# Operand addresses of TensorE modulo 64 bytes in a one-core encoder trunk: one residue for all, low tiles moved

## The chip, the core and the metric

One core of a Trainium2 chip runs the whole program. The metric is the device time of one execution in microseconds (us), the median of the timed runs. For the kernel before that is 1330.88 us (three runs, 1330.51 to 1332.0). Five engines work in parallel, each with an instruction queue of its own: PE (TensorE, matmuls; its weight loads are listed apart as PEld), DVE (VectorE), ACT (ScalarE), POOL (GpSimd) and SP (which only issues DMAs here).

## What is computed

One layer of an encoder over 256 tokens of width 2048, in float32, cut here to its matmuls:

```python
h = rms_norm(x, g_norm)
proj = h @ w_in                                  # 2048 x 9216: u,v | q,k,v | two gates
y_a = gmlp_branch(uv, ln_g, ln_b, w_s, b_s)      # u * (W_s LN(v) + b), by 128-token chunks
y_b = neighbourhood_attn(q, k, v, rpb)           # 16 heads
merged = g_a * (y_a @ w_branch[:GM_WIDTH]) + g_b * (y_b @ w_branch[GM_WIDTH:])
x = x + merged @ w_out
up = conv3(rms_norm(x, g) @ w_up)                # 2048 x 11008, then a width-3 convolution over tokens
x = x + (silu(gate) * val) @ w_down              # 5504 x 2048
return rms_norm(x, norm_final)
```

## The kernel before

**Two parts for each operand.** Every big product is made from float32 operands split in two: a high part (rounded to the matmul's format, tiles `whi` and `half_hi` for weights, written by ACT at L245) and a low part, the rest (`wlo`, `half_lo`, written by DVE at L248). Three products are added in PSUM: high x high, high x low, low x high.

**Weights arrive in pieces.** All weight matrices lie in HBM in the order of use, cut into pieces of at most 512 KB. `load` sends one piece by one DMA from SP's queue into a free `wraw` tile (the first 16 pieces, which hold a part of x beside their weights, into `start` tiles). `prepare` splits pieces up to `AHEAD - 1` = 4 ahead of the one in use, each into a slot of two tiles, `whi` and `wlo`, of 128 partitions x 1024 elements. Slots 0 to 3 lie at the low end of SBUF; from the output projection on there are also slots 4 and 5 and the pair `half_hi`/`half_lo`, at the high end. A slot returns to the end of a list when its piece has been used. `begin(i)` loads, prepares, and then runs the tasks that were put down for piece i with `at(i, f)`; after it the matmuls of piece i follow. So the order of work on each engine is fixed by this loop.

**Kinds of groups.** In a matmul the moving operand is streamed (up to 512 columns) against a stationary operand of 128 x 128 that a LDWEIGHTS has loaded before.

- Weight-stationary groups (`ws_step`, `spread_products`): u, q/k and the up-projection. The weights are stationary, the activations `h` move. L349 multiplies a high weight tile with both parts of `h` (512 columns), L355 a low weight tile with the high part alone (256 columns). Even pieces run all highs first and then all lows, odd pieces lows first, so highs and lows come in runs of 16. There are 1760 of each; 1376 of each belong to the up-projection.
- Groups with moving weights (`three_products`, L364 to L366, 908 matmuls on each line, 512 columns): v, gates, branches, output projection, down-projection. Stationary are `h`, `y` (branch outputs), `m` (merged) or `a` and `s` (activations of the MLP).
- The first group (L381, L382, L384, 192 matmuls), v of the gMLP, whose pieces bring x.

**Down-projection.** Some pairs of its pieces are multiplied with seven products in place of eight; L301 to L304 build sums of weights, and `combine` (L460 to L463 and L958, DVE and ACT) adds the parts up afterwards, in three tasks that are put down for the three pieces after the pair. In the last group the last four pieces are multiplied output by output (`by_block`), so that each finished output can be normalised and stored while PE goes on.

**Start.** ACT's queue sends the x part of piece 0 and then the 8 KB of norm weights (`vec`, L548); SP sends the rest of piece 0 in two DMAs, and the next pieces. PE runs 14 transposes of the identity meanwhile (`WAKE`, L561).

**Addresses.** Where a tile starts in its partition, modulo 64 bytes (in the text: its residue), as the built program has it:

```
tile                                            before   after
whi, slots 0 to 3 (low end of SBUF)                  0      32
wlo, slots 0 to 3                                    0      32 (start of the tile)
h, a, s, m, wraw, start, ident (low end)             0      32
whi and wlo, slots 4 and 5 (high end)               32      32 (start of the tile)
half_hi, half_lo, y, x2 (high end)                  32      32
```

Before, all low-end tiles in this table stand at 256 modulo 512, all high-end ones at 480 modulo 512. Tiles are cut at multiples of 512 bytes for a matmul's operands.

Of the kernel before, what the change touches and what calls it, by code (L numbers as in the profile page):

```python
# [8 lines left out]
F32 = mybir.dt.float32  # L9
F32R = mybir.dt.float32r  # L10
# [5 lines left out]
T = 256  # L16
D = 2048
NT = T // 128
KD = D // 128
# [20 lines left out]
BLOCK = 1024  # L40
AHEAD = 5
RAW, UNITS, HALVES = 5, (4, 2), 1
WAKE = 14
EARLY = 4

FF_BLOCKS = ((0, 22), (22, 43))
FF_SEVEN = ((3, 5, 7), (2, 4, 6))
# [71 lines left out]
def weight_pieces():  # L119

    groups, order = weight_stream()
    out, count, at = [], {}, 0
    for key in order:
        _, w, pieces = groups[key]
        tiles, blocks = pieces[count.get(key, 0)]
        count[key] = count.get(key, 0) + 1
        cols = sum(n for _, n in blocks)
        out.append((key, w, tiles, blocks, at, cols))
        at += 128 * len(tiles) * cols
    return out, at  # L130
# [19 lines left out]
def trunk_kernel(ctx, tc, x, weights, vectors, ln_g, ln_b, w_s_turned, b_s, rpb, norm_final, out):  # L150
    nc = tc.nc
# [8 lines left out]
    def keep(name, side="left", bufs=1, space=None):  # L160
        p, st = pool(name, side, bufs, space)
        ctx.push(st)
        return p

    psum = keep("psum", space=PSUM)
    const = keep("const")
# [3 lines left out]
    ypool, y_st = pool("yT", "right")  # L170

    junk = tmp.tile([128, 512], F32, name="junk")

    banks = {n: None for n in range(8)}
    spare = list(range(8))

    def bank():
        n = spare.pop(0)
        banks[n] = psum.tile([128, 512], F32, name=f"bank{n}")
        return banks[n]  # L180
# [7 lines left out]
    pieces, _ = weight_pieces()  # L188
# [17 lines left out]
    def at(i, f):  # L206
        tasks.setdefault(i, []).append(f)
# [5 lines left out]
    def load():  # L213
        while n_loaded[0] < len(pieces):
            i = n_loaded[0]
            slots = start_free if i < KD else raw_free
            if not slots:
                return
            n_loaded[0] += 1
            for f in preload.pop(i, ()):  # L220
                f()
            _, _, tiles, _, off, cols = pieces[i]
            size = len(tiles) * cols
            slot = slots.pop(0)
            w = slot[0].tile([128, size if i < KD else BLOCK], F32, name=slot[1])
            for c0, c1 in ((T, 768), (0, T), (768, 1280)) if i == 0 else ((0, size),):
                queue = nc.scalar if (i, c0) == (0, 0) else nc.sync
                queue.dma_start(w[:, c0:c1], bass.AP(tensor=weights.tensor, offset=weights.offset + off + c0,
                                                       ap=[[size, 128], [1, c1 - c0]]))
            raw[i] = (w, slot)  # L230

    def raw_done(i):
        (start_free if i < KD else raw_free).append(raw.pop(i)[1])

    def unit(key):
        slot = unit_free.pop(0)
        h, l = (slot[0].tile([128, BLOCK], F32R, name=f"w{p}{slot[1]}") for p in ("hi", "lo"))
        units[key] = (h, l, slot)
        return h, l

    def unit_done(key):
        unit_free.append(units.pop(key)[2])

    def high(h, w):
        nc.scalar.activation(h, w, AF.Copy)  # L245

    def low(l, w, h):
        nc.vector.tensor_sub(l, w, h.bitcast(F32))  # L248

    def split_first(i):  # L250
        def go():
# [6 lines left out]
            else:  # L258
                nc.scalar.activation(dst[:, 0, :], x, AF.Copy, scale=g)
            nc.vector.scalar_tensor_tensor(dst[:, 1, :], x, g, dst[:, 0, :].bitcast(F32), op0=OP.mult,  # L260
                                           op1=OP.subtract)
            parts = ((0, 512), (512, 1024)) if i < EARLY else ((0, 1024),)
            for c0, c1 in parts:
# [5 lines left out]
    def split_piece(i):  # L269
        if i < KD:  # L270
            return split_first(i)

        def go():
            size = len(pieces[i][2]) * pieces[i][5]
            h, l = unit(i)
            w = raw[i][0]
            high(h[:, :size], w[:, :size])
            low(l[:, :size], w[:, :size], h[:, :size])
            raw_done(i)
        return go  # L280
# [38 lines left out]
    queue = []  # L319
# [104 lines left out]
    def wide_step(key, acts, sevens, rest, done, by_block=0):  # L424


        n0, size = starts[key], size_of[key]
        tiles = [pieces[n0 + n][2][0] for n in range(size)]
        firsts = [n for n in range(size) if n0 + n in seven]
        box, opened, left = {}, set(), {}  # L430
        OUT = {(0, 0): 2, (0, 1): 3, (1, 0): 4, (1, 1): 8}
        uses = []
        n = 0
        while n < size:
            if n in firsts:
                uses += [1, 2, 3, 5, 7, 6, 4]
                n += 2
            else:
                uses += list(OUT.values())
                n += 1  # L440
        for u in uses:
            left[u] = left.get(u, 0) + 1

        def p(u):
            if u not in box:
                box[u] = bank()
            return box[u]

        def product(u, x, w):
            start = u not in opened  # L450
            opened.add(u)
            left[u] -= 1
            three_products(p(u), x, w, start, left[u] == 0)

        def combine(i):

            nu, nv = (fx["p"].tile([128, 512], F32, name=f"comb{n}") for n in range(2))

            def one():
                nc.scalar.activation(nu, p(1), AF.Copy)  # L460
                rest(0, 0, nu, OP.add)
                nc.vector.tensor_sub(nu, nu, p(6))
                nc.vector.tensor_sub(nv, nu, p(7))  # L463
                free(p(1), p(6), p(7))

            def two():
                rest(0, 1, nu, OP.subtract)
                rest(0, 1, p(5), OP.add)
                rest(1, 0, nv, OP.add)

            def three():
                rest(1, 1, nv, OP.subtract)
                rest(1, 1, p(5), OP.add)
                free(p(5))

            for n, f in enumerate((one, two, three)):
                at(i + 1 + n, f)

        def step(i):
            n = i - n0  # L480
            c0, c1 = slice(0, 512), slice(512, 1024)
            if n in firsts:
                k = tiles[n]
                h, l, _ = halves[i]
                hb, lb, _ = units[i, "b"]
                product(1, acts(k, 0), (h, l))
                product(2, acts(k + 1, 0), (hb[:, c0], lb[:, c0]))
                product(3, sevens(k)[3], (hb[:, c1], lb[:, c1]))
                half_free.append(halves.pop(i)[2])
                unit_done((i, "b"))  # L490
            elif n - 1 in firsts:
                k = tiles[n - 1]
                ht, lt, _ = units[i - 1, "t"]
                hs, ls, _ = units[i - 1, "s"]
                S = sevens(k)
                product(5, S[0], (ht[:, c0], lt[:, c0]))
                product(7, S[2], (ht[:, c1], lt[:, c1]))
                unit_done((i - 1, "t"))
                product(6, S[1], (hs[:, c1], ls[:, c1]))
                product(4, acts(k + 1, 1), (hs[:, c0], ls[:, c0]))  # L500
                unit_done((i - 1, "s"))
                if n - 1 == firsts[-1]:
                    combine(i)
            elif n < size - by_block:
                h, l, _ = units[i]
                for (b, c), u in OUT.items():
                    cs = slice(c * 512, (c + 1) * 512)
                    product(u, acts(tiles[n], b), (h[:, cs], l[:, cs]))
                unit_done(i)
            elif n == size - 1:  # L510
                for b, c in ((0, 0), (1, 0), (0, 1), (1, 1)):
                    u = OUT[b, c]
                    for m in range(size - by_block, size):
                        h, l, _ = units[n0 + m]
                        cs = slice(c * 512, (c + 1) * 512)
                        product(u, acts(tiles[m], b), (h[:, cs], l[:, cs]))
                    done(p(u), b, c, i + 1)
                    free(p(u))
                for m in range(size - by_block, size):
                    unit_done(n0 + m)  # L520
            if n == size - 1 and not by_block:
                for (b, c), u in OUT.items():
                    done(p(u), b, c, i + 1)
                    free(p(u))
        return step
# [18 lines left out]
    vec = const.tile([128, 2 * KD + 8 * NF], F32)  # L544
    gmix, gffn = vec[:, :KD], vec[:, KD:2 * KD]
    ck = vec[:, 2 * KD:].rearrange("p (j f) -> p j f", j=4)
    load()
    nc.scalar.dma_start(gmix, vectors[:, :KD])  # L548

    one = const.tile([128, 1], F32)  # L550
    nc.vector.memset(one, 1.0)
# [10 lines left out]

    keep_awake(WAKE)
    free(wake)
# [588 lines left out]
    for n in range(len(FF_BLOCKS)):  # L1153
        for j in range(2):
            key = ("down", n, j)
# [110 lines left out]
    for i, piece in enumerate(pieces):  # L1266
        key = piece[0]
# [45 lines left out]
```

## Time and profile before

The profiled execution took 1331.57 us; its span, from the first to the last instruction, is 1329.1 us.

| engine | busy | instructions |
|---|---|---|
| PEld | 1116.5 us (84%) | 6778 |
| ACT | 728.8 us (55%) | 1072 |
| POOL | 100.3 us (8%) | 192 |

Weight DMAs on SP's queue move 252.33 MB and keep the 16 DMA engines 59.0% busy. "Busy" of PE is from the start of a matmul to its modelled end; matmuls overlap, so the pace of PE is read from the distance of two starts, not from the mean duration of one. A row of the timeline has the start in us from the span's start, the duration (of the merged instructions, if there are several, with their count behind x), engine, line, operation, output and inputs, and in brackets the idle time before it and what ended that. Buffer numbers are left out of its names.

### The profile page before, as it was taken

Reading aid. Unit: us, or ns where it says so; the run is one execution under the profiler, and the core shown is the slowest. Engines: PE = TensorE matmul, PEld = TensorE weight load, DVE = VectorE, ACT = ScalarE, POOL = GpSimd, SP = SyncE. Lnnn points to the kernel's source line nnn. Section 1 sums busy time; section 2 is a strip of 40 time slices with the busy share of each in tenths; the row PEclk is TensorE's granted clock in tenths of the full one; section 3 lists DMA queues with packets and bytes.
Section 4 is the critical chain, followed back from the end, with each engine's and each line's share of the span. In section 5 each row is a group of like instructions: output and inputs, shape, how many; then the busy total and the mean of one; then the engine's idle time right before and its main releaser. Section 6 shows DMA issues by size and latency. Waiting matters only on the chain.

```text
span 1329.1 us, 18475 instructions
## 1 busy us (share of the span) xinstructions
PE 1316.1 (99%) x6778; PEld 1116.5 (84%) x6778; DVE 945.4 (71%) x1362; ACT 728.8 (55%) x1072; POOL 100.3 (8%) x192
## 2 busy tenths in 40 slices
PE   9999999999999999999999999999999999999996
PEld 7888888888788888888888888888888888888885
DVE  5676667776564546565878777797858787869986
ACT  5855567576444444454655555554545555546553
POOL 0502065430000000000000000000000000000000
PEclk9999999999999999999999999999999999999999
DMA  8857676655556667665565656556656565546743
GB/s 327 321 177 208 195 218 191 203 151 190 180 182 189 190 189 255 204 189 187 171 203 174 200 179 199 180 175 220 207 190 190 191 187 194 183 135 222 249 147 127
DMA packets 73898, 261.40 MB, mean 197 GB/s; under 512 B 9552, under 2 KB 10832, under 8 KB 73296
## 3 DMA queue, kind: packets, MB, share of 16 engines
q1 hardware_dynamic: 69696, 252.33, 59.0%
q0 software_dynamic: 3680, 7.30, 2.0%
q8 instruction: 53, 0.87, 0.3%
q10 hardware_dynamic: 432, 0.60, 0.1%
q14 instruction: 37, 0.30, 0.1%
HBM read 256.00 MB, written 2.10 MB: 194 GB/s over the span
## 4 chain that ended last, share of the span: by engine, by line
PE 95%; DVE 3%; DMA 1%; ACT 1%; issue 0%; ACTq 0%; DVEq 0%
PE bank L349 30%; PE bank L355 16%; PE bank L364 14%; PE bank L366 14%; PE bank L365 14%; PE bank L381 1%; PE bank L382 1%; PE bank L384 1%; DVE wlo L248 1%; DMA wraw<-in_weights_dram 1%; PE bank L830 1%; ACT whi L245 0%; PE bank L882 0%; DMA vec<-in_vectors_dram 0%; PE bank L704 0%
## 5 line engine op out<-in xcount | busy, mean ns | idle before, releaser
L248 DVE TENSOR_TENSOR wlo<-wraw,whi 128x1024 fp32r<-128x1024 f32 (+1 forms) x466 | 561.2, 1217 | 231.1 <-ACT whi L245 223.5
L245 ACT ACTIVATE whi<-wraw 128x1024 fp32r<-128x1024 f32 (+1 forms) x466 | 481.1, 1046 | 285.2 <-PE bank L365 168.9
L349 PE MATMUL bank<-h,whi 128*128 128x512 f32 x1760 | 425.8, 392 | 0.0
L349 PEld LDWEIGHTS bank<-h,whi 128*128 128x128 f32 x1760 | 322.2, 188 | 64.1
L355 PEld LDWEIGHTS bank<-h,wlo 128*128 128x128 f32 x1760 | 225.3, 190 | 9.4
L355 PE MATMUL bank<-h,wlo 128*128 128x256 f32 x1760 | 229.5, 282 | 0.0
L364 PE MATMUL bank<-whi,h 128*128 128x512 f32 x320 | 126.0, 394 | 0.0
L366 PE MATMUL bank<-wlo,h 128*128 128x512 f32 x320 | 124.8, 390 | 0.0
L365 PE MATMUL bank<-whi,h 128*128 128x512 f32 x320 | 124.6, 389 | 0.0
L366 PE MATMUL bank<-wlo,a 128*128 128x512 f32 x248 | 97.2, 392 | 0.8 <-DVE wlo L248 0.8
L364 PE MATMUL bank<-whi,a 128*128 128x512 f32 x248 | 97.2, 392 | 0.0
L365 PE MATMUL bank<-whi,a 128*128 128x512 f32 x248 | 97.2, 392 | 0.0
L1020 ACT ACTIVATE tc<-ta,vec 128x256 f32<-128x256 f32 x86 | 47.1, 595 | 84.4 <-DVE ta L1018 84.4
L696 DVE TENSOR_TENSOR ta<-bank,tb 128x256 f32<-128x256 f32 x110 | 39.0, 417 | 67.6 <-ACT tb L694 67.6
L694 ACT ACTIVATE tb<-bank 128x256 f32<-128x256 f32 x110 | 36.2, 384 | 90.9 <-PE bank L349 86.2
L366 PEld LDWEIGHTS bank<-wlo,h 128*128 128x128 f32 x320 | 60.1, 188 | 12.8
L364 PEld LDWEIGHTS bank<-whi,h 128*128 128x128 f32 x320 | 60.1, 188 | 12.3
L365 PEld LDWEIGHTS bank<-whi,h 128*128 128x128 f32 x320 | 60.1, 188 | 12.0
L366 PEld LDWEIGHTS bank<-wlo,a 128*128 128x128 f32 x248 | 46.6, 188 | 11.6 <-DVE wlo L248 1.3
L364 PEld LDWEIGHTS bank<-whi,a 128*128 128x128 f32 x248 | 46.6, 188 | 10.3
L365 PEld LDWEIGHTS bank<-whi,a 128*128 128x128 f32 x248 | 46.6, 188 | 10.3
L1260 POOL DMA_DIRECT2D h<-in_norm_final_dram x4 | 2.2, 539 | 680.0 <-DVE wlo L248 679.5
(182 smaller groups left out, 1465.8 us busy)
## 6 DMA issues: line engine op xcount, KB each, us to landing
wraw<-in_weights_dram SPq DMA_DIRECT2D x446, 512.0 KB, 4.3
start<-in_weights_dram SPq DMA_DIRECT2D x15, 640.0 KB, 6.5
xs<-in_x_dram SPq DMA_DIRECT2D x2, 1024.0 KB, 9.5
vw<-va POOLq DMA_DIRECT2D x32, 64.0 KB, 5.3
x<-in_x_dram POOLq DMA_DIRECT2D x2, 1024.0 KB, 9.3
wraw<-in_weights_dram SPq DMA_DIRECT2D x8, 256.0 KB, 2.9
run<-in_rpb_dram POOLq DMA_DIRECT2D x64, 31.2 KB, 4.2
out_dram<-x SPq DMA_DIRECT2D x5, 256.0 KB, 2.8
```

Of the source, the lines that this page charges most:

```text
L245: nc.scalar.activation(h, w, AF.Copy)
L248: nc.vector.tensor_sub(l, w, h.bitcast(F32))
L349: nc.tensor.matmul(p, h[:, c:c + 128], acts(2 * n + k), start=n == 0 and k == 0, stop=last and k == tiles - 1)
L355: nc.tensor.matmul(p[:, :T], l[:, c:c + 128], acts(2 * n + k)[:, 0, :], start=False, stop=False)
L364: nc.tensor.matmul(p, xh, wh, start=start, stop=False)
L365: nc.tensor.matmul(p, xl, wh, start=False, stop=False)
L366: nc.tensor.matmul(p, xh, wl, start=False, stop=stop)
L381: nc.tensor.matmul(p, xh, h[:, cs], start=n == 0, stop=False)
L382: nc.tensor.matmul(p, xl, h[:, cs], start=False, stop=False)
L694: nc.scalar.activation(t, p[:, T:], AF.Copy)
L696: nc.vector.tensor_add(a, p[:, :T], t)
L1020: nc.scalar.activation(v, u, AF.Identity, scale=ck[:, 1, ch:ch + 1], bias=ck[:, 3, ch:ch + 1])
```

## The change

```diff
-WAKE = 14
+WAKE = 18
 EARLY = 4
+LINE = 16
+LOW_AT = {("u", 0): 4, ("u", 1): 12, ("qk", 0): 2, ("qk", 1): 6, ("qk", 2): 1, ("qk", 3): 10}
+LOW_AT_UP = 8
...
     junk = tmp.tile([128, 512], F32, name="junk")
+    const.tile([128, 8], F32, name="line")
...
-            for c0, c1 in ((T, 768), (0, T), (768, 1280)) if i == 0 else ((0, size),):
-                queue = nc.scalar if (i, c0) == (0, 0) else nc.sync
-                queue.dma_start(w[:, c0:c1], bass.AP(tensor=weights.tensor, offset=weights.offset + off + c0,
+            for c0, c1 in ((0, 768), (768, 1280)) if i == 0 else ((0, size),):
+                nc.sync.dma_start(w[:, c0:c1], bass.AP(tensor=weights.tensor, offset=weights.offset + off + c0,
                                                        ap=[[size, 128], [1, c1 - c0]]))
...
-    def unit(key):
+    def unit(key, low_at=0):
         slot = unit_free.pop(0)
-        h, l = (slot[0].tile([128, BLOCK], F32R, name=f"w{p}{slot[1]}") for p in ("hi", "lo"))
+        h = slot[0].tile([128, BLOCK], F32R, name=f"whi{slot[1]}")
+        l = slot[0].tile([128, BLOCK + LINE], F32R, name=f"wlo{slot[1]}")[:, low_at:low_at + BLOCK]
...
-            size = len(pieces[i][2]) * pieces[i][5]
-            h, l = unit(i)
+            size, key = len(pieces[i][2]) * pieces[i][5], pieces[i][0]
+            h, l = unit(i, LOW_AT_UP if key[0] == "up" else LOW_AT.get(key, 0))
...
             for n, f in enumerate((one, two, three)):
-                at(i + 1 + n, f)
+                at(i + 3 if by_block else i + 1 + n, f)
...
+    nc.scalar.dma_start(gmix, vectors[:, :KD])
     load()
-    nc.scalar.dma_start(gmix, vectors[:, :KD])
```

**Addresses.** A 32-byte tile in the constants' pool moves every tile of the low end behind it by 32 bytes, to the residue of the high end. A `wlo` tile has 64 bytes more, and the low part begins in it 32 bytes on for the up-projection (residue 0), and for the two u groups and the four q/k groups 16, 48, 8, 24, 4 and 40 bytes on; for all other pieces it begins at the tile's start. The 64 bytes also move each following slot: slots 0 to 3 start at 288, 352, 416 and 480 modulo 512, slots 4 and 5 at 352 and 416, and `h`, `a`, `s` and `m` all at 32.

**Start.** First instructions of ACT's queue before (`start0` is piece 0's tile, 128x256 its x part):

```order
L228 DMA start0_86<-in_weights_dram 128x256
L548 DMA vec_85<-in_vectors_dram 128x16
L554 ACT_TABLE_LOAD
L554 ACTIVATE one_97<-one_97 128x1
L245 ACTIVATE whi0_157<-start0_86 128x512 x2
```

and after, line numbers being three or four higher:

```order
L551 DMA vec_86<-in_vectors_dram 128x16
L558 ACT_TABLE_LOAD
L558 ACTIVATE one_97<-one_97 128x1
L249 ACTIVATE whi0_161<-start0_88 128x512 x2
L263 ACTIVATE h1_120<-start1_91,vec_86 128x256
```

The norm weights are now ACT's first DMA, and x comes with the first 512 weight columns in one DMA of SP (128x768 before 128x512, where two of 128x512 stood). PE has 18 transposes ahead of its first product in place of 14.

**End.** DVE in the last group, from the split of its third last piece to the first finished output (`x_4961`, the tile x2, is the sum that becomes the output, `comb` and `bank` hold the parts that `combine` adds), before:

```order
L248 TENSOR_TENSOR wlo_12126<-wraw_12072,whi_12125 128x1024
L958 TENSOR_TENSOR x_4961<-x_4961,comb_12123 128x512
L462 TENSOR_TENSOR comb_12123<-comb_12123,bank_11962 128x512
L463 TENSOR_TENSOR comb_12124<-comb_12123,bank_11958 128x512
L248 TENSOR_TENSOR wlo_12146<-wraw_12074,whi_12145 128x1024
L958 TENSOR_TENSOR x_4961<-x_4961,comb_12123 128x512
L958 TENSOR_TENSOR x_4961<-x_4961,bank_11954 128x512
L958 TENSOR_TENSOR x_4961<-x_4961,comb_12124 128x512
L248 TENSOR_TENSOR wlo_12165<-wraw_12092,whi_12164 128x1024
L958 TENSOR_TENSOR x_4961<-x_4961,comb_12124 128x512
L958 TENSOR_TENSOR x_4961<-x_4961,bank_11954 128x512
L964 TENSOR_TENSOR x_4961<-bank_11848,x_4961 128x512
```

and after:

```order
L252 TENSOR_TENSOR wlo_12130<-wraw_12076,whi_12129 128x1024
L252 TENSOR_TENSOR wlo_12146<-wraw_12078,whi_12145 128x1024
L252 TENSOR_TENSOR wlo_12162<-wraw_12096,whi_12161 128x1024
L962 TENSOR_TENSOR x_4965<-x_4965,comb_12127 128x512
L466 TENSOR_TENSOR comb_12127<-comb_12127,bank_11966 128x512
L467 TENSOR_TENSOR comb_12128<-comb_12127,bank_11962 128x512
L962 TENSOR_TENSOR x_4965<-x_4965,comb_12127 128x512
L962 TENSOR_TENSOR x_4965<-x_4965,bank_11958 128x512
L962 TENSOR_TENSOR x_4965<-x_4965,comb_12128 128x512 x2
L962 TENSOR_TENSOR x_4965<-x_4965,bank_11958 128x512
L968 TENSOR_TENSOR x_4965<-bank_11852,x_4965 128x512
```

The last two splits now stand ahead of the eight additions, which follow in one block directly before the first finished output. Elsewhere the order of instructions is the same.

## The prediction

> **What bounds the kernel now.** I read the page's first part, then the chain of work that ended last, then the waits of PE.
>
> ```profile
> span 1329.1 us, 18475 instructions
> PE 1316.1 (99%) x6778; PEld 1116.5 (84%) x6778; DVE 945.4 (71%) x1362; ACT 728.8 (55%) x1072; POOL 100.3 (8%) x192
> PE 95%; DVE 3%; DMA 1%; ACT 1%; issue 0%; ACTq 0%; DVEq 0%
> PE bank L366 <- DVE wlo L248: 0.8, 1, 0.8
> PE bank L381 <- DVE h L257: 1.0, 1, 1.0
> ```
>
> PE is busy all the time, 95% of the chain is its own, and it waits twice, 1.8 us in all. So the time is the sum of PE's steps from one matmul start to the next, plus a start and a tail. What remains to be found is whether those steps are as short as they can be. For that I compare stages that run the same instruction with operands at different addresses. First, gate groups (stationary `h`, moving `whi`, both at residue 0) beside a branch group (stationary `y`, at residue 32): starts from the timeline, counts from the groups by line in the same two windows.
>
> ```profile
> 389.27 0.48 PE L364 MATMUL bank<-whi,h 128*128 128x512 f32 x1
> 427.47 0.39 PE L364 MATMUL bank<-whi,y 128*128 128x512 f32 x1
> 449.86 0.39 PE L364 MATMUL bank<-whi,h 128*128 128x512 f32 x1
> L364 PE MATMUL bank<-whi,h 128*128 128x512 f32 x56 | 21.9, 391 | 0.0
> L364 PE MATMUL bank<-whi,y 128*128 128x512 f32 x32 | 12.6, 395 | 0.0
> ```
>
> The three lines L364 to L366 have equal counts, so 168 matmuls take 427.47 - 389.27 = 38.20 us, **227.4 ns** each, and 96 take 449.86 - 427.47 = 22.39 us, **233.2 ns** each. In the down-projection the moving side differs instead: the first four products use slot 2 (residue 0), the next 24 matmuls slots 4 and 5 (residue 32), all against `a` at 0.
>
> ```profile
> 854.86 0.39 PE L364 MATMUL bank<-whi,a 128*128 128x512 f32 x1
> 857.58 0.40 PE L364 MATMUL bank<-whi,a 128*128 128x512 f32 x1
> 863.19 0.39 PE L364 MATMUL bank<-whi,a 128*128 128x512 f32 x1
> ```
>
> 12 matmuls in 2.72 us are 226.7 ns each; 24 in 5.61 us are 233.8. Last, the up-projection, where the weights are stationary and `h` (residue 0) moves.
>
> ```profile
> 700.51 2.08 PE L355 MATMUL bank<-h,wlo 128*128 128x256 f32 x16
> 702.42 3.82 PE L349 MATMUL bank<-h,whi 128*128 128x512 f32 x16
> 706.08 2.05 PE L355 MATMUL bank<-h,wlo 128*128 128x256 f32 x16
> 707.96 3.90 PE L349 MATMUL bank<-h,whi 128*128 128x512 f32 x16
> 711.70 0.98 PE L355 MATMUL bank<-h,wlo 128*128 128x256 f32 x7
> ```
>
> Highs at residue 0 (slots 1 and 2): 3.66 us for 16, 228.8 ns. Highs at 32 (slots 4 and 5): 3.74 us, 233.8. **Lows go the other way**: 16 at residue 0 take 1.91 us, 119.4 ns; 16 of which half stand at 32 take 1.88 us, 117.5. So 512-column steps like equal residues of moving and stationary, 256-column steps a distance of 32.
>
> To get sums I laid the addresses of the built program beside all of PE's starts. By the difference between the residue of the next stationary operand and that of the operand moving just then, steps over 250 ns left out: moving-weight lines 1835 steps at difference 0, mean 227.2 ns, and 859 at 32, mean 233.4; highs 1208 at 0, 228.8, and 426 at 32, 233.5; lows 1214 at 0, about 119.3, and 425 at 32, 117.3. The rows above are members of these classes.
>
> **The change, part by part.**
>
> *Residues of the moving-weight lines.* Afterwards `y`, the high slots, `h`, `a`, `s`, `m` and the low slots all stand at 32, so all differences are 0: 859 x 6.2 ns = 5.3 us. The means at 0 still hold slow steps just after a switch from 32 (22 ns in all over five steps after the row at 863.19); with no switch left these go too, 1835 x (227.2 - 226.7) = 0.9 us. Together **6.2 us**.
>
> *Highs.* 426 steps lose 233.5 - 228.8 = 4.7 ns: **2.0 us**. I keep 228.8, not 226.7, since a run of highs still begins after a run of lows, and its first five steps are the slow ones there.
>
> *Lows.* In the up-projection they now stand 32 bytes off `h` in every slot: 862 steps gain 2.0 ns, 1.7 us. In u and q/k, 352 steps get differences of 16, 48, 8, 24, 4 and 40 bytes, which no row shows. The nearest rows are lows at 32 (single steps of 113 to 120 ns) and, on the bad side, what a wrong difference costs a high (+6): between -2.2 and +2.1 us. I take the value at 32, -0.7. Together **2.4 us**. A run's border from high to low now costs as at 32 (231 for 227 ns, 88 borders) and from low to high gains the same (116 for 120); these cancel.
>
> On the moved rows a rule of the skill can be weighed. The Trainium skill, "TensorE: Matmul & The Clock Gate", section "Wait — 56ns, not 53.3ns?", gives a step of N / 2.4 + 2.5 ns for a warm array, and N / 1.2 for a cold one. The cold one agrees with this trace (426.7 by the page, 0.43 us between the rows at 8.75 and 9.18 below); warm, the trace has 226.7 ns where the page gives 215.7. If the moved lows ran at the page's 109.2 ns, their term would be about 12 us in place of 2.4, by an estimate from that page.
>
> *DVE, ACT and DMAs* write the moved tiles, and read them. The group of low splits and the stage in which DVE is fullest (columns: span of the window, then busy time and count of PE, PEld, DVE, ACT, POOL):
>
> ```profile
> L248 DVE TENSOR_TENSOR wlo<-wraw,whi 128x1024 fp32r<-128x1024 f32 (+1 forms) x466 | 561.2, 1217 | 231.1 <-ACT whi L245 223.5
> 854.86:971.85 116.99, 116.99 (x511) 95.74 (x510) 101.04 (x122) 60.77 (x70) 0.00 (x0) 1.00 0.60 198
> ```
>
> Split by slot, the 1024-element low split takes 1228 ns to slots 0 to 3 and 1221 to slots 4 and 5, so writes at residue 32 cost nothing. DVE is 86% busy in that stage; PE gets about 1.4% faster there (239 steps of 507 by 6.5 ns), DVE comes to 88%, and PE's wait is still covered. Cost: nothing. If DVE were the bound, PE would wait on L248 all over, and only the two waits above are there.
>
> *Start.*
>
> ```profile
> 0.75 0.40 ACTq L228 DMA_DIRECT2D start<-in_weights_dram  x1
> 1.18 0.46 ACTq L548 DMA_DIRECT2D vec<-in_vectors_dram  x1
> 5.10 0.35 DVE L257 TENSOR_SCALAR h<-start,vec 128x256 fp32r<-128x256 f32 x1 [4.22 <-DMA vec<-in_vectors_dram]
> 1.37 3.25 PE L561 MATMUL bank<-ident 128*128 128x128 f32 x14 [1.37 <-POOL ident masks.py:199]
> 5.60 0.77 PE L381 MATMUL bank<-whi,h 128*128 128x512 f32 x1 [0.98 <-DVE h L257]
> 8.75 0.63 PE L382 MATMUL bank<-whi,h 128*128 128x512 f32 x1
> 9.18 0.63 PE L381 MATMUL bank<-whi,h 128*128 128x512 f32 x1
> 8.24 0.51 ACT L259 ACTIVATE h<-start,vec 128x256 fp32r<-128x256 f32 x1 [2.81 <-DMA start<-in_weights_dram]
> 9.30 1.29 DVE L248 TENSOR_TENSOR wlo<-start,whi 128x512 fp32r<-128x512 f32 x2
> 10.37 0.39 PE L381 MATMUL bank<-whi,h 128*128 128x512 f32 x1
> ```
>
> The first product waits for `vec`, which is now issued at 0.75 in place of 1.18: 0.43 us earlier, if the larger DMA of x and weights is there by then. PE still steps 0.43 us per matmul (half pace) at 9.18, and reaches piece 1 at 10.37. Piece 1's parts are ready about 9.30 whatever PE does, so the start gains at most 1.07 us. The 14 transposes end at 4.6, so 18 end at 5.4 to 5.5: PE is no longer idle before its first product, and the half pace may end sooner; the last transposes may hold that product up to 5.3. Between 0.3 and 1.07 I take **0.8 us**; 0 if the DMA comes late.
>
> *End.* The seventh-product additions stood between the last splits and held PE up:
>
> ```profile
> 1303.02 1.23 DVE L248 TENSOR_TENSOR wlo<-wraw,whi 128x1024 fp32r<-128x1024 f32 x1 [1.08 <-ACT whi L245]
> 1309.34 1.22 DVE L248 TENSOR_TENSOR wlo<-wraw,whi 128x1024 fp32r<-128x1024 f32 x1
> 1309.38 0.39 PE L365 MATMUL bank<-whi,a 128*128 128x512 f32 x1
> 1310.61 0.50 PE L366 MATMUL bank<-wlo,a 128*128 128x512 f32 x1 [0.84 <-DVE wlo L248]
> 1311.80 0.68 DVE L964 TENSOR_TENSOR x<-bank,x 128x512 f32<-128x512 f32 x1
> 1313.88 0.69 DVE L964 TENSOR_TENSOR x<-bank,x 128x512 f32<-128x512 f32 x1 [0.27 <-PE bank L366]
> 1316.63 0.69 DVE L1098 TENSOR_TENSOR x<-bank,x 128x512 f32<-128x512 f32 x1 [0.86 <-PE bank L366]
> 1319.38 0.68 DVE L1098 TENSOR_TENSOR x<-bank,x 128x512 f32<-128x512 f32 x1
> ```
>
> The step from 1309.38 takes 1.23 us, and the next one is 0.11 long too: 1.1 us. With the splits first that goes. What is late next is DVE: the same eleven operations from 1303.02 end at 1311.8, or up to 0.5 later if the last split waits for ACT, and the four outputs follow them. DVE had 0.27 + 0.86 us of waits for PE in that stretch, all of which PE's gain can use: between 0.4 and 1.1, I take **0.8 us**.
>
> Sum: 6.2 + 2.0 + 2.4 + 0.8 + 0.8 = **12.2 us**. The profiled execution took 1331.57 us, 0.69 above the median, so 1319.4 by it and 1318.7 by the median. I say **1319.0**.
>
> **Rivals.**
>
> 1. *Not the residue but the region.* In every row above the operand at 32 also lies at the high end of SBUF. If crossing to that end makes the 233 ns, a move of 32 bytes changes no step, and only start and end stay: 1331.57 - 1.6 = 1330.0. For it: the two never come apart before. Against it: lows get faster there, by 2 ns, which a longer way would hardly do. The Trainium skill, "SBUF — State Buffer", section "Who interferes with whom", says that PE has independent read ports for moving and stationary operands and never waits on anyone; by that rule no address would matter, and the result would be the same. The 227.4 and 233.2 above do not fit it.
>
> 2. *Slower: the 64-byte steps.* The wider `wlo` sets slots 1 to 5 at other distances from `h`, `a` and `y` modulo 128 and more; before, all equal residues were equal modulo 512. If the pattern repeats every 128 bytes, slots 1, 3 and 4 (half the steps) go at the slow pace: 2164 steps in place of 1285, 879 x 5.7 ns = + 5.0, less the lows' 2.4 and the 1.6 of start and end: 1332.6, still the same. If every 256 or more, five slots in six, 3607 steps, + 13.2 less 4.0 = + 9.2: **1340.8**. It decides against the change once the repeat is over 128 bytes. Against it: `y` stands 224 bytes off the moving slots and slots 4 and 5 stand 288 off `a`, 96 and 32 modulo 128, yet 233.2 and 233.8 ns are alike.
>
> 3. *Smaller.* Lows gain nothing, or the borders between runs cost more with lows moved (five slow steps, up to 25 ns, twice in each run, on some 90 runs), or the odd offsets cost 2 us: 1323 to 1328.
>
> 4. *Larger.* The moved lows all settle near their shortest step, 113 ns: 1214 x 4 ns more, and the first steps of the runs of highs go: 1310 to 1316.
>
> **How the numbers follow.** Forecast (1316 to 1323) 0.57; larger 0.10; smaller 0.15; region 0.08; 64-byte steps with a repeat of 128 bytes 0.03, of more 0.07. The range takes in the forecast, larger and smaller, 0.82, and leaves rivals 1 and 2 out: 1310 to 1328. About 0.2%, 2.7 us, is what a measurement of this kernel can tell from no change; 1328.2 is the border. Faster: forecast, larger and smaller, 0.82. Same: region and a repeat of 128, 0.11. Slower: 0.07.
>
> **What would show it.** Branch groups and down-projection at 226.7 ns a step throughout: the residue is right; 233 in slots 4 and 5 alone: the region; 233 in slots 1 and 3: the 64-byte steps. Highs at 16 steps in 3.66 us in every slot, lows at 16 in 1.88 or less. A first product at 5.2 and piece 1 before 10. No step over 0.3 us in the last group, with DVE's last L1098 row 0.4 to 1.1 us nearer to PE's last matmul. The forecast is wrong if the step rows do not change with the residues, or if lows in u and q/k get slower than 120 ns.

## The result and the profile after

The changed kernel takes 1337.36 us (median of 6 runs, 1336.98 to 1337.72) where the kernel before takes 1331.55 (6 runs): ratio 1.0044, 95% interval 1.0031 to 1.0057. It is slower, by 5.8 us. The profiled execution took 1337.72 us.

The page's first part, the chain and the waits of PE in the changed kernel:

```profile
span 1335.6 us, 18480 instructions
PE 1323.4 (99%) x6782; PEld 1115.9 (84%) x6782; DVE 945.4 (71%) x1362; ACT 728.8 (55%) x1072; POOL 100.5 (8%) x192
PE 97%; DMA 2%; DVE 1%; ACT 0%; issue 0%; SPq 0%; DVEq 0%; ACTq 0%
PE bank L385 <- ACT whi L249: 0.9, 1, 0.9
```

PE is still all of it, DVE and ACT are as busy as before, and no wait is left at the end. So PE's steps have become longer. The starts that were read before, now for gate groups and a branch group (L368 is L364 of before; 168 and 96 matmuls as there):

```profile
391.60 0.48 PE L368 MATMUL bank<-whi,h 128*128 128x512 f32 x1
430.57 0.40 PE L368 MATMUL bank<-whi,y 128*128 128x512 f32 x1
452.80 0.39 PE L368 MATMUL bank<-whi,h 128*128 128x512 f32 x1
860.18 0.40 PE L368 MATMUL bank<-whi,a 128*128 128x512 f32 x1
862.98 0.40 PE L368 MATMUL bank<-whi,a 128*128 128x512 f32 x1
868.53 0.39 PE L368 MATMUL bank<-whi,a 128*128 128x512 f32 x1
```

Gates: 38.97 us for 168, **232.0 ns** a step where it was 227.4. Branch: 22.23 us for 96, 231.6 where it was 233.2. Down-projection: slot 2 takes 2.80 us for 12, 233.3 (it was 226.7), slots 4 and 5 take 5.55 us for 24, 231.3 (it was 233.8). What was slow got a little faster, and **what was fast, more than twice as many steps, got slow**. The up-projection (L353 highs, L359 lows):

```profile
690.44 3.89 PE L353 MATMUL bank<-h,whi 128*128 128x512 f32 x16
694.17 2.06 PE L359 MATMUL bank<-h,wlo 128*128 128x256 f32 x16
696.07 3.88 PE L353 MATMUL bank<-h,whi 128*128 128x512 f32 x16
699.79 2.05 PE L359 MATMUL bank<-h,wlo 128*128 128x256 f32 x16
701.68 3.83 PE L353 MATMUL bank<-h,whi 128*128 128x512 f32 x16
705.35 0.87 PE L359 MATMUL bank<-h,wlo 128*128 128x256 f32 x6
```

Two runs of highs take 3.73 and 3.72 us (233 ns a step), one 3.67 (229): by the addresses of the program the first two use slots that stand 64 and 128 bytes off `h` modulo 256, the third slots at 192 and 0. Lows take 1.90 and 1.89 us a run, 118.5 ns.

With addresses laid beside all starts as in the prediction (steps over 250 ns left out), the 512-column steps of the changed kernel sort by the distance of the next stationary operand from the moving one, modulo 256 bytes. Moving-weight lines have 229.1 ns at distance 0, 232.9 at 64, 232.7 at 128 and 230.3 at 192. Against `h`, `a`, `s` and `m` these are slot 0, slot 3, slots 2 and 5, and slots 1 and 4. In the up-projection, where the weights are the stationary side, the sign turns round: highs have 229.5 ns in slot 0 (distance 0), 233.2 and 232.7 in slots 1 and 4 (64), 232.4 in slots 2 and 5 (128) and 229.7 in slot 3 (192). All these distances are 0 modulo 64. That is the prediction's second rival.

Times by stage, from matmul start to matmul start, in us of the profiled executions, here and for the experiments below. The first group is counted from its second piece, the first half of the up-projection over its last 1328 matmuls, and the last group over the last 195 matmuls of the program.

| stage | before | after | no steps | one distance | low 224 | as meant |
|---|---|---|---|---|---|---|
| first group | 40.80 | 42.24 | 40.94 | 40.93 | 40.95 | 40.84 |
| gates 389 to 427 | 38.20 | 38.98 | 38.18 | 38.18 | 38.18 | 38.18 |
| branch 427 to 450 | 22.39 | 22.22 | 21.97 | 21.76 | 21.76 | 21.76 |
| up-projection, first half | 231.58 | 232.30 | 230.22 | 231.11 | 229.44 | 231.39 |
| down-projection, first half | 116.99 | 117.89 | 117.02 | 115.60 | 115.60 | 115.61 |
| last group | 45.91 | 44.91 | 44.61 | 43.97 | 43.97 | 43.99 |

About 0.5 us of the 42.24 is not a matter of addresses. In this execution a piece of the first group came later from its DMA than in the kernel that keeps the steps alone (below): ACT takes it up at 29.92 in place of 29.27, and twice PE's weight load waits for its splits.

```profile
29.92 0.51 ACT L263 ACTIVATE h<-start,vec 128x256 fp32r<-128x256 f32 x1 [2.63 <-DMA start<-in_weights_dram]
31.43 0.19 PEld L385 LDWEIGHTS bank<-whi,h 128*128 128x128 f32 x1 [0.34 <-ACT whi L249]
32.69 0.19 PEld L388 LDWEIGHTS bank<-wlo,h 128*128 128x128 f32 x1 [0.50 <-DVE wlo L252]
```

With the steps alone the first group takes 41.73.

### The profile page after: what moved, and what is told of

It is laid out like the page before. It is cut to its first block, busy times and chain, and to the rows that moved or that the text cites. A ratio compares the mean times of both kernels' runs of the same rounds, so it can differ in the third digit from the quotient of the medians.

```text
span 1335.6 us, 18480 instructions
## 1 busy us (share of the span) xinstructions
PE 1323.4 (99%) x6782; PEld 1115.9 (84%) x6782; DVE 945.4 (71%) x1362; ACT 728.8 (55%) x1072; POOL 100.5 (8%) x192
## 4 chain that ended last, share of the span: by engine, by line
PE 97%; DMA 2%; DVE 1%; ACT 0%; issue 0%; SPq 0%; DVEq 0%; ACTq 0%
PE bank L353 31%; PE bank L368 16%; PE bank L370 16%; PE bank L359 16%; PE bank L369 16%; DMA start<-in_weights_dram 2%; PE bank L834 1%; PE bank L388 1%; PE bank L386 0%; PE bank L385 0%; PE bank L886 0%; PE bank L708 0%; DVE wlo L252 0%; PE bank L875 0%; PE bank L995 0%; PE bank L935 0%
## 5 line engine op out<-in xcount | busy, mean ns | idle before, releaser
L252 DVE TENSOR_TENSOR wlo<-wraw,whi 128x1024 fp32r<-128x1024 f32 (+1 forms) x466 | 560.8, 1216 | 235.1 <-ACT whi L249 226.3
L353 PE MATMUL bank<-h,whi 128*128 128x512 f32 x1760 | 428.6, 394 | 0.0
L353 PEld LDWEIGHTS bank<-h,whi 128*128 128x128 f32 x1760 | 322.1, 188 | 66.1
L359 PEld LDWEIGHTS bank<-h,wlo 128*128 128x128 f32 x1760 | 224.5, 188 | 9.9
L359 PE MATMUL bank<-h,wlo 128*128 128x256 f32 x1760 | 228.6, 281 | 0.0
L368 PE MATMUL bank<-whi,h 128*128 128x512 f32 x320 | 127.3, 398 | 0.0
L368 PE MATMUL bank<-whi,a 128*128 128x512 f32 x248 | 97.6, 394 | 0.0
L368 PEld LDWEIGHTS bank<-whi,h 128*128 128x128 f32 x320 | 60.2, 188 | 13.2
L368 PEld LDWEIGHTS bank<-whi,a 128*128 128x128 f32 x248 | 46.6, 188 | 10.7
```

The lines of the kernel that those rows point to most:

```text
L353: nc.tensor.matmul(p, h[:, c:c + 128], acts(2 * n + k), start=n == 0 and k == 0, stop=last and k == tiles - 1)
L359: nc.tensor.matmul(p[:, :T], l[:, c:c + 128], acts(2 * n + k)[:, 0, :], start=False, stop=False)
L368: nc.tensor.matmul(p, xh, wh, start=start, stop=False)
```

## Experiments

Each is built on the changed kernel unless it says otherwise, and timed beside the kernel before (1331.07 us in the first set, 1331.24 in the second).

**Without the steps and the moved low parts.**

```diff
-LINE = 16
-LOW_AT = {("u", 0): 4, ("u", 1): 12, ("qk", 0): 2, ("qk", 1): 6, ("qk", 2): 1, ("qk", 3): 10}
-LOW_AT_UP = 8
+LINE = 0
+LOW_AT = {}
+LOW_AT_UP = 0
```

> The change without the 64 extra bytes of a low tile and without the moved low parts: every operand at residue 32, all low-end tiles at 288 modulo 512, all high-end tiles at 480. Theory A, the distance of the next stationary operand from the moving one counts modulo 512 (or 256, 128) and only 0 is fast: steps between two low-end tiles (2033 with moving weights, 1296 highs) go back to 226.7 to 229 ns, while those across the ends, now 192 bytes apart (859 with moving weights, 454 highs), stay at 229 to 234; with the start and the end of the change that is 1326 to 1330 us. Theory B, the residue 32 itself is slow for an operand: everything stays at 229 to 234 ns, about 1337 us. Theory C, only the distance modulo 64 counts and the moved low parts disturb the highs beside them: all 512-column steps at 227, about 1321 us.

Measured: 1325.1 us, ratio 0.9955 (0.9943 to 0.9968). Everything stands at residue 32, yet steps within the low end are back at 227.3 (moving weights, 2025 steps) and 228.7 ns (highs). So residue 32 is not slow in itself: theory B falls. Across the ends it depends on the sign. A branch group and slots 4 and 5 of the down-projection:

```profile
425.81 0.39 PE L368 MATMUL bank<-whi,y 128*128 128x512 f32 x1
447.78 0.39 PE L368 MATMUL bank<-whi,h 128*128 128x512 f32 x1
853.73 0.39 PE L368 MATMUL bank<-whi,a 128*128 128x512 f32 x1
859.33 0.39 PE L368 MATMUL bank<-whi,a 128*128 128x512 f32 x1
```

96 steps in 21.97 us, 228.9 ns, with the stationary operand 192 bytes on from the moving one; 24 in 5.60 us, 233.3, with it 320 on (64 modulo 256). Both are 0 modulo 64, so theory C falls too, and theory A stands. The time is 0.9 us under the 1326 that theory A gave as its least. Part of that is in the up-projection, whose first half is faster here than with any other kernel but one: in slots 4 and 5 both parts stand 192 bytes on from `h`, and there highs have 228.9 ns and lows 116.1, where the other slots have 228.7 and 120.0. Runs of 16 lows and 16 highs, in turn:

```profile
669.86 2.02 PE L359 MATMUL bank<-h,wlo 128*128 128x256 f32 x16
671.72 3.82 PE L353 MATMUL bank<-h,whi 128*128 128x512 f32 x16
675.37 2.06 PE L359 MATMUL bank<-h,wlo 128*128 128x256 f32 x16
677.27 2.91 PE L353 MATMUL bank<-h,whi 128*128 128x512 f32 x12
```

In both runs of lows half stand at 0 and half at 192, yet one takes 1.86 us and the other 1.90. Lows in slot 4, which follow lows at 0, have 113.9 ns; those in slot 5, which follow highs, 117.6. So the distance is not all: what goes ahead counts too, as the scans below show for highs.

**One distance for all.** As the last one, and:

```diff
-    const.tile([128, 8], F32, name="line")
+    const.tile([128, 56], F32, name="line")
```

> As the run without steps, but the tile in the constants has 224 bytes, so that low-end and high-end tiles both stand at 480 modulo 512 and every distance is 0 modulo 512. Theory A: all 512-column steps near 227 ns, lows at 120, 859 x 6.2 + 426 x 5 ns less than before and the start and end of the change: 1320 to 1323 us. Theory B (residue 32 itself is slow): 229 to 234 ns everywhere, about 1337 us. Theory D (the high end of SBUF is slow, whatever the address): steps with slots 4 and 5 and with y stay at 233, about 1329 us.

Measured: 1323.0 us, ratio 0.9940 (0.9927 to 0.9954). Gates and branch:

```profile
387.02 0.48 PE L368 MATMUL bank<-whi,h 128*128 128x512 f32 x1
425.20 0.39 PE L368 MATMUL bank<-whi,y 128*128 128x512 f32 x1
446.96 0.39 PE L368 MATMUL bank<-whi,h 128*128 128x512 f32 x1
```

168 steps in 38.18 us, 227.3, and 96 in 21.76, **226.7**. Over the whole run the moving-weight lines have 226.9 ns, slots 4 and 5 included. The high end of SBUF is as fast as the low end: theory D, the prediction's first rival, falls.

**Scan of the low parts, and of the high parts.** With one distance for all, the low tiles are 512 bytes wider and the low part stands at another place in each of the 22 groups; in the second kernel the same for the high parts.

```diff
-LINE = 0
-LOW_AT_UP = 0
+LINE = 128
+AT_UP = {0: 0, 2: 4, 4: 8, 6: 12, 8: 16, 10: 24, 12: 32, 14: 40, 16: 48, 18: 56, 20: 64, 22: 72, 24: 80, ...}
...
-            h, l = unit(i, LOW_AT_UP if key[0] == "up" else LOW_AT.get(key, 0))
+            h, l = unit(i, AT_UP[key[1]] if key[0] == "up" else 0)
```

> All operands at 480 modulo 512 and a low tile 512 bytes wider (so slots keep their place modulo 512); in each of the 22 up-projection groups the low part stands another number of bytes on: 0, 16, 32, 48, 64, 96, and so on to 480, and 4, 8, 40, 496. Theory A expects a step of lows that changes with the offset over the whole 512 bytes, 120 ns at 0, 115 to 120 elsewhere; a period of 64 bytes would give the same step at 32, 96, 160 and 224. A theory in which only residue 64 counts for lows gives 117 at 32, 96, 160, 224, 288 and so on, and 120 at multiples of 64.

> The same scan for the high parts of the up-projection, low parts at distance 0. Theory A: 227 ns at offset 0 alone (and perhaps near it), 229 at 256, 233 at 64 and 320, 232 at 128 and 384, 230 at 192 and 448, as the changed kernel has them in its slots 0 to 3; theory B: the same step at every offset that is 0 modulo 64, and another one at 32 modulo 64.

Measured: one run each, 1321.17 and 1327.32 us. Lows at 224 bytes (807.23) and at 256 bytes (834.89) in the first kernel; a run lasts to the start of the next row:

```profile
807.23 2.03 PE L359 MATMUL bank<-h,wlo 128*128 128x256 f32 x16
809.09 3.82 PE L353 MATMUL bank<-h,whi 128*128 128x512 f32 x16
...
834.89 2.08 PE L359 MATMUL bank<-h,wlo 128*128 128x256 f32 x16
836.80 3.82 PE L353 MATMUL bank<-h,whi 128*128 128x512 f32 x16
```

1.86 us at 224, 1.91 at 256. Highs at 64 bytes and at 256 in the second kernel:

```profile
704.54 3.90 PE L353 MATMUL bank<-h,whi 128*128 128x512 f32 x16
708.27 2.06 PE L359 MATMUL bank<-h,wlo 128*128 128x256 f32 x16
...
834.05 3.82 PE L353 MATMUL bank<-h,whi 128*128 128x512 f32 x16
837.70 2.08 PE L359 MATMUL bank<-h,wlo 128*128 128x256 f32 x16
```

3.73 us at 64, 3.65 at 256. All offsets, as the time of 64 highs and 64 lows of a group (us; each step counted with at most 240 and 130 ns, so that stalls stay out; the values at an offset and at 256 bytes more). The 22.27 at 0 is that of a group in the run with one distance, since the scans' own group at 0 is the first of the up-projection, has interruptions by transposes in it and takes 22.30:

| distance, bytes | lows moved | highs moved |
|---|---|---|
| 0 / 256 | 22.27 / 22.27 | 22.27 / 22.30 |
| 32 / 288 | 22.29 / 22.29 | 22.51 / 22.50 |
| 64 / 320 | 22.16 / 22.16 | 22.54 / 22.54 |
| 96 / 352 | 22.13 / 22.13 | 22.60 / 22.60 |
| 128 / 384 | 22.27 / 22.27 | 22.48 / 22.47 |
| 160 / 416 | 22.32 / 22.32 | 22.60 / 22.60 |
| 192 / 448 | 22.28 / 22.28 | 22.38 / 22.38 |
| 224 / 480 | 22.12 / 22.12 | 22.55 / 22.55 |
| 4, 8, 16 | 22.19, 22.13, 22.26 | 22.47, 22.38, 22.53 |
| 40, 48 | 22.22, 22.22 | 22.55, 22.54 |

The pattern **repeats every 256 bytes**, to 0.01 us but for one pair; the 512 of theory A was only a bound. Highs are fastest at 0, and of the places tried only 8 and 192 bytes come within 0.12 us of it. With lows moved, a group gains some 0.15 us at 8, 96 and 224 bytes and nothing at 128, 160 and 192, and 32 bytes is one of the places without a gain: lows take 118.2 ns there in place of 119.5, but the highs after them 230.1 in place of 228.4. Each scan moves one part and leaves the other at 0; as the run without steps shows, the two do not simply add when both are moved.

**Only the steps.** The changed kernel with `LOW_AT = {}` and `LOW_AT_UP = 0`, `LINE = 16` kept.

> The changed kernel with the 64-byte steps of the slots kept and no low part moved inside its tile. If the steps are the loss: 1336 to 1339 us, with 229, 233, 232 and 230 ns in slots 0 to 3 as in the changed kernel. If the moved low parts did it: near the run without steps, 1325 us.

Measured: 1335.11 us, ratio 1.0031 (1.0019 to 1.0042). It is 10.0 us above the run without steps, and 0.9 us under the range that was expected: **the 64 extra bytes are the loss**. By distance, the steps of the moving-weight lines are those of the changed kernel to 0.1 ns. With the low parts moved as well the time is 2.3 us longer (1337.36); 1.9 us of that lie in the two halves of the up-projection (231.29 and 234.08 us here, 232.30 and 234.99 in the changed kernel), where the steps and the offsets put the lows at 32, 96, 160 and 224.

**As it was meant.** The low parts moved as in the change, but steps of a whole period.

```diff
-LINE = 16
+LINE = 64
...
-    const.tile([128, 8], F32, name="line")
+    const.tile([128, 56], F32, name="line")
```

> The changed kernel, low parts moved as there (32 bytes in the up-projection; 16, 48, 8, 24, 4, 40 in the other weight-stationary groups), but with a low tile 256 bytes wider in place of 64, and all operands at 224 modulo 256. If the 64-byte steps were the whole loss: all 512-column steps with moving weights at 227 ns. The prediction's term for lows says 2.4 us less than the run with one distance, 1320.6 us; the scan says that highs give back what lows gain at 32 bytes (22.29 us a group against 22.27), so 1322.5 to 1323.5.

Measured: 1322.36 us, ratio 0.9936 (0.9924 to 0.9949), between the two expectations, 0.1 us from that of the scan. In the up-projection, where lows stand at 32, it is slower than the run with one distance by 0.28 and 0.26 us in the two halves (the first is in the table by stages). In u and q/k together it is 0.27 us faster. So the term for lows is not there. The 0.6 us by which its median is lower lie within the spread of the run with one distance (1321.86 to 1324.14). Highs and lows in it:

```profile
691.71 3.84 PE L353 MATMUL bank<-h,whi 128*128 128x512 f32 x16
695.39 2.05 PE L359 MATMUL bank<-h,wlo 128*128 128x256 f32 x16
697.28 3.84 PE L353 MATMUL bank<-h,whi 128*128 128x512 f32 x16
```

Lows 1.89 us, 0.02 less than at distance 0; highs 3.68, about 0.03 more.

**Start and end alone.** The kernel before with `WAKE = 18`, the two transfers of piece 0, the norm weights first, and the three tasks of `combine` together; no address moved.

> The kernel before with only the start (norm weights first, two transfers of piece 0, 18 transposes) and the end (the three tasks of the additions together) of the change; no address moves. The prediction's terms say 0.8 + 0.8 us less than before, the two traces (piece 1 is reached 1.3 us earlier, the last group is 1.0 us shorter) 2.0 to 2.4 us less: 1328.7 to 1329.5 us. If what the start gains is lost again to the loads of the next pieces, about 1330.

Measured: 1328.72 us, ratio 0.9983 (0.9974 to 0.9991), 2.5 us less than before. The last group takes 44.52 us for 45.91, and piece 1 is reached at 8.87, 1.5 us earlier than before (L380 and L381 are L381 and L382 of the kernel before):

```profile
5.70 0.39 PE L381 MATMUL bank<-whi,h 128*128 128x512 f32 x1
8.87 0.50 PE L380 MATMUL bank<-whi,h 128*128 128x512 f32 x1 [0.48 <-ACT whi L244]
```

Both edits are a gain that the changed kernel has too, and loses again to its longer steps.

**Low parts 224 bytes on.** One distance for all, `LINE = 64`, and the low part at 56 elements in all weight-stationary groups.

```diff
+LINE = 64
+LOW_AT = {(n, j): 56 for n in ("u", "qk") for j in range(4)}
+LOW_AT_UP = 56
```

> All operands at 224 modulo 256, low tiles 256 bytes wider, and the low part 224 bytes on in all weight-stationary groups. Theory A with a period of 256 bytes: 512-column steps with moving weights as in the run with one distance (226.9 ns), a group of 128 up-projection steps at 22.12 us in place of 22.27, some 24 to 27 such groups: 1318 to 1320 us. If the period is 512, slots 1 and 3 (256 bytes off) get slower than 227 ns: 1325 or more.

Measured: **1318.34 us**, ratio 0.9906 (0.9891 to 0.9921), better than both kernels. Two runs each:

```profile
690.45 3.82 PE L353 MATMUL bank<-h,whi 128*128 128x512 f32 x16
694.11 2.03 PE L359 MATMUL bank<-h,wlo 128*128 128x256 f32 x16
695.98 3.82 PE L353 MATMUL bank<-h,whi 128*128 128x512 f32 x16
699.64 2.03 PE L359 MATMUL bank<-h,wlo 128*128 128x256 f32 x16
```

Highs 3.66 us a run, lows 1.87, with slots 256 bytes apart modulo 512: the period is 256 here too.

## Why the prediction was wrong, step by step

- **Residues of the moving-weight lines (6.2 us): the step that failed.** It took "all stand at 32, so all differences are 0" as if only the remainder modulo 64 counted. The distance counts modulo 256, and the change sets five of six slots off it. The prediction had this as its second rival, at 1340.8 us and 0.07; that price was 3.4 us too high. What it held against it was that distances of 224 and 288 bytes had the same price. The scan shows why that said nothing: 32 and 224 modulo 256 are both slow, and so is all between them. That a row existed only at 0 and at plus and minus 32 was no ground for a period of 64.
- The size of that term is right for a kernel that does what the step assumed: with one distance the moving-weight steps have 226.9 ns (226.7 forecast).
- **Highs (2.0 us): the same.** With one distance they have 228.6 ns (228.8 forecast); in the changed kernel a run of 16 takes 3.72 us in slots 4 and 5, where it took 3.73, and 3.73 in slots 1 and 2, where it took 3.65.
- **Lows (2.4 us): failed for a second reason.** The fast lows of before stood in slots 4 and 5, 224 bytes on from `h`, not 32; the two were taken for one because they are equal modulo 64. At 32 the following highs give the gain back, as the third rival feared; at 224 it is kept (229.44 us for 231.11 in the first half). On top of the 64-byte steps the moved lows cost 1.9 us in the up-projection.
- **DVE, ACT, DMAs (nothing): right.** The low split has 1216 ns after, 1217 before, and nothing in PE's waits names it. The one time that a weight load waits for a low split, 0.50 us in the first group, the cause is the late piece shown above.
- **Start (0.8 us) and end (0.8): right in kind, too small.** Together 2.5 us alone. In the changed kernel's start:

```profile
5.13 0.55 PE L385 MATMUL bank<-whi,h 128*128 128x512 f32 x1
5.53 0.39 PE L386 MATMUL bank<-whi,h 128*128 128x512 f32 x1
5.75 0.39 PE L385 MATMUL bank<-whi,h 128*128 128x512 f32 x1
7.99 0.51 ACT L263 ACTIVATE h<-start,vec 128x256 fp32r<-128x256 f32 x1 [2.59 <-DMA start<-in_weights_dram]
9.07 0.50 PE L385 MATMUL bank<-whi,h 128*128 128x512 f32 x1 [0.86 <-ACT whi L249]
```

The first product starts at 5.13 (5.17 by the working), steps are at full pace from 5.53 on, and piece 1 becomes the bound, as said. But its data came 0.25 us earlier than before (7.99 for 8.24), so it was reached at 9.07, 1.3 us earlier, past the bound of 1.07. At the end the step of 1.23 us is gone, and DVE keeps pace: its first output follows the additions at once, and by the third it waits for PE again. The prediction's sign for the end, DVE's last such row nearer to PE's last matmul, could not show anything: DVE's row starts 0.43 us after the start of that matmul in both kernels. The gain lies in PE's own time for the last group (44.52 us for 45.91 with start and end alone).

```profile
1318.35 0.68 DVE L968 TENSOR_TENSOR x<-bank,x 128x512 f32<-128x512 f32 x1
1323.02 0.69 DVE L1102 TENSOR_TENSOR x<-bank,x 128x512 f32<-128x512 f32 x1 [0.89 <-PE bank L370]
1325.80 0.69 DVE L1102 TENSOR_TENSOR x<-bank,x 128x512 f32<-128x512 f32 x1
```

- **The first rival** (the region) fell with the run with one distance. With it the prediction weighed the Trainium skill, "SBUF — State Buffer", section "Who interferes with whom", which says that PE's two read ports are independent and that PE never waits on anyone. Read as the prediction read it, that no address would matter, it does not hold here: by address alone a group of the up-projection takes 22.12 to 22.60 us. Whether the ports have to do with it no run shows.

## What to carry to other kernels

When a busy PE is the bound, compare the step between matmul starts of the same instruction at different operand addresses, and lay out the tiles so that the distance between moving and stationary operands is under control in all buffers of a ring: one odd pad moves every later buffer. Rows at two or three distances do not tell the period; before relying on one, scan it, which costs one kernel if each group of a long loop gets its own offset. And look at what follows the steps that get faster: the lows' gain at 32 bytes was lost again in the highs behind them.

## What the runs showed of the hardware that was not expected

- The step between two float32r matmuls depends on the distance of stationary and moving operand modulo 256 bytes: 226.7 ns at 0 and up to about 234 elsewhere with 512 columns; with 256 columns, among highs at distance 0, 119.5 at 0, 116.1 at 8, 116.6 at 224, 120.3 at 128.
- It depends also on what goes ahead: in the run without steps lows at 192 have 113.9 ns behind lows at 0 and 117.6 behind highs at 192.
- The same place in the same order gives the same time, to a nanosecond or two over a run of 16 matmuls: lows at 224 took 1.865 us in each of eight runs, at 0 and 256 1.912 or 1.913 in the up-projection.
- After a run of the other kind it takes a step or several to settle: a run of 16 highs at distance 0 takes 3.65 us after lows at 0, not 16 x 226.7 = 3.63.
- With 18 transposes, up to the first product, PE was at full pace from 5.53 us on; with 14 and a gap of 1 us it still had a step of 0.43 us at 9.18. Number and gap changed together, so the runs do not tell which of them did it.

Two things stay open. The sums sort steps by the next stationary and the present moving operand, and that pair alone does not set the step. In the scan of the lows the last high of a run, at distance 0 itself, takes 226 ns when the low behind it stands at 64 bytes and 235 when it stands at 32 or 224. In the scan of the highs the last high at 64 takes 234 though the low behind it stands at 0. So both the next operand and what went before count; how they combine no run here tells. Nor does any tell why 256 bytes, or why 226.7 is the least.
